# RMS normalisation on one core: the first three tiles' loads move to ScalarE's DMA queue, in few large transfers

## The chip, the core and the metric

The kernel runs on one core of a Trainium2 chip. A core has engines that run side by side, each with its own stream of instructions: TensorE (PE in the profile), VectorE (DVE), ScalarE (ACT), GpSimd (POOL) and SyncE (SP). SyncE does no arithmetic here: it issues transfers between the chip's memory (HBM) and the core's own memory (SBUF). ScalarE can issue transfers too, between its arithmetic. All transfers are carried by 16 DMA engines. The metric is the device time of one execution in microseconds (us).

## The reference

The input `x` has 16 x 1024 rows of 512 numbers in float32, 33.6 MB; the output has the same size. Every row is divided by its root mean square and multiplied by `gamma`, a vector of 512 numbers:

```python
eps = 1e-5
rms = np.sqrt(np.mean(x ** 2, axis=-1, keepdims=True) + eps)
return (x / rms * gamma).astype(np.float32)
```

## The kernel before

The 16384 rows are cut into four tiles of 4096: 128 partitions with 32 rows each. The rows of one partition are neighbours in HBM, so a transfer of 16 rows of each partition (half a tile, 4 MB) is made of 128 pieces of 32 KB. There are three buffers in SBUF (`slots`), each of one whole tile. Tiles 0, 1 and 2 have one each; tile 3 goes into tile 0's slot, and its loads wait until tile 0's stores have read that slot. Results overwrite the input in its slot and are stored from there.

The work goes by groups of rows, mostly half tiles. For a group:

- ScalarE squares its rows in pieces (L96) and VectorE sums each piece (L97) into `ss`. The pieces go in turn to a buffer in PSUM of seven rows and one in SBUF of five. A piece of nine rows, used for the first three half tiles, is squared into rows 23 to 31 of slot 2, whose own load comes late.
- ScalarE takes the root of the mean (L102), VectorE the reciprocal (L103).
- GpSimd takes the last `share` rows, seven of 16 mostly, and multiplies them by the reciprocal (L109) and by gamma (L110).
- ScalarE multiplies the other rows by the reciprocal, one instruction a row (L118), and VectorE multiplies them by gamma (L122).

The order on every engine is the order in which the kernel is written (`manual_schedule`). While group k is scaled, ScalarE already squares group k+1: two pieces ahead of the first half of its scaling, the rest between the halves. At the start, TensorE spreads gamma over the partitions with a matrix product (L66) and ScalarE copies it to SBUF (L165).

Before the change, SyncE issues every transfer, and its queue carries them out in the order of issue. It starts with row 0 of tile 0, rows 1 to 7, gamma in five pieces, rows 8 to 15, rows 16 to 31, and the first half of tile 1. Everything else is issued by `transfers`, after the group that is named there: after group (0, 0), stores of one row alternate with the second half of tile 1 and rows 0 to 22 of tile 2; after group (0, 16), which comes with both halves of tile 0 done, the rest of tile 2's load, the stores of tile 0 and the loads of tile 3. A store waits for VectorE's and GpSimd's products; a load into a slot that is still in use waits for the store from it. An issue that waits holds up those behind it on SyncE. L34 holds an address alignment of ScalarE's instructions, at the very start of its stream; L72 is a first activation that brings in ScalarE's table.

Of the kernel before, what the change touches and what calls it, by code (L numbers as in the profile page):

```python
# [9 lines left out]
def kernel(  # L10
# [6 lines left out]
    nc = tc.nc  # L17
    P = nc.NUM_PARTITIONS
    eps = 1e-5
    fp32 = mybir.dt.float32  # L20
# [5 lines left out]
    N, D = xf.shape  # L26
# [3 lines left out]
    xv = xf.rearrange("(t p r) d -> t p r d", p=P, r=R)  # L30
# [5 lines left out]
    const = ctx.enter_context(tc.tile_pool(name="const", bufs=1))  # L36
    stats = ctx.enter_context(tc.tile_pool(name="stats", bufs=9))
    psum = ctx.enter_context(tc.tile_pool(name="psum", bufs=1, space=bass.MemoryType.PSUM))

    slots = [const.tile([P, R, D], fp32, name=f"slot{i}") for i in range(3)]  # L40
# [1 line left out]
    before_scale = []  # L42

    def load(t, slot, r0, r1):
        dma = nc.sync.dma_start(out=slots[slot][:, r0:r1], in_=xv[t][:, r0:r1])  # L45
        before_scale.append((slot, r0, r1, dma))

    def store(t, slot, r0, r1):
        dma = nc.sync.dma_start(out=ov[t][:, r0:r1], in_=slots[slot][:, r0:r1])
        before_scale.append((slot, r0, r1, dma))  # L50

    gamma_row = const.tile([1, D], fp32)
    pieces = (0, 128, 224, 320, 416, D)

    load(0, 0, 0, 1)
    load(0, 0, 1, 8)
    for c0, c1 in zip(pieces, pieces[1:]):
        nc.sync.dma_start(out=gamma_row[:, c0:c1], in_=gamma.unsqueeze(0)[:, c0:c1])
    load(0, 0, 8, 16)
    load(0, 0, 16, 32)  # L60
    load(1, 1, 0, 16)

    ones_col = const.tile([1, P], fp32)
    nc.gpsimd.memset(ones_col, 1.0)  # L64
# [9 lines left out]


    groups = [
        (0, 0, 7, (7,), 3),
        (0, 7, 9, (9,), 5),
        (0, 16, 16, (7, 9), 7),
        (1, 0, 16, (7, 9), 7),  # L80
        (1, 16, 16, (7, 5, 4), 7),
        (2, 0, 16, (7, 5, 4), 7),
        (2, 16, 16, (7, 5, 4), 7),
# [3 lines left out]
    slot_of = [0, 1, 2, 0]  # L87

    def square_sums(ss, t, g, r, m, k):
        if m == 9:  # L90
            sq = slots[2][:, 23:32, :]
        else:
            home, name, most = ((psum, "sq_psum", 7), (const, "sq_sbuf", 5))[k % 2]
            sq = home.tile([P, most, D], fp32, name=name)
        rows = slots[slot_of[t]][:, g + r : g + r + m, :]
        nc.scalar.activation(out=sq[:, :m], in_=rows, func=AF.Square)  # L96
        nc.vector.tensor_reduce(  # L97
            out=ss[:, r : r + m, 0], in_=sq[:, :m], axis=mybir.AxisListType.X, op=OP.add
        )
# [28 lines left out]

    def transfers(t, g):
        if (t, g) == (0, 0):  # L130
            store(0, 0, 0, 1)
            load(1, 1, 16, 32)
            store(0, 0, 1, 2)
            load(2, 2, 0, 23)
        elif (t, g) == (0, 16):
            store(0, 0, 2, 3)
            load(2, 2, 23, 32)
            store(0, 0, 3, 16)
            store(0, 0, 16, 32)
            load(3, 0, 0, 16)  # L140
            load(3, 0, 16, 32)
        elif (t, g) == (1, 16):
            store(1, 1, 0, 32)
        elif (t, g) == (2, 16):
            store(2, 2, 0, 32)
        elif (t, g) == (3, 0):
            store(3, 0, 0, 16)
        elif (t, g) == (3, 16):
            store(3, 0, 16, 32)
# [12 lines left out]
    for piece in todo:  # L162
        square_sums(*piece)
    rstd = inverse_rms(ss, groups[0][2])
    nc.scalar.copy(out=gamma_b[:, 0], in_=gamma_psum[:, 0])  # L165
    for k, group in enumerate(groups):
        t, g, n, pieces, share = group
        mine = n - share
        half = (mine + 1) // 2
        ahead = groups[k + 1 :][:1]  # L170
        ss, todo = pieces_of(ahead[0]) if ahead else (None, [])
        scale_by_pool(rstd, t, g, n, share)
        for piece in todo[:2]:
            square_sums(*piece)
        scale(rstd, t, g, 0, half)
        for piece in todo[2:]:
            square_sums(*piece)
        scale(rstd, t, g, half, mine)
        times_gamma(t, g, 0, mine)
        transfers(t, g)  # L180
        for nxt in ahead:
            rstd = inverse_rms(ss, nxt[2])
# [30 lines left out]
```

## Time and profile before

| what | value |
|---|---|
| device time, median of 3 runs | 161.59 us (161.41 to 161.67) |
| the profiled execution's own time, as recorded: its span, first to last instruction | 160.2 us |
| the median over that span | 1.4 us |
| VectorE, ScalarE, GpSimd busy | 112.0, 107.8, 106.4 us (70%, 67%, 66%) |
| TensorE busy | 2.0 us |
| moved by DMA | 67.12 MB, 419 GB/s over the span |

For the profiled execution the record has no device time apart from its span, so sums are made against the span and the 1.4 us is added. In the profile, a name such as L97 is line 97 of the kernel. A group's row shows the instruction, the tile written and the tiles read, the count, and behind the bar the busy time in us and the mean of one in ns, then the engine's idle time before them and what ended it. A "q" behind an engine's name (SPq) is its sequencer, which issues transfers and waits. A row of the timeline begins with start and length in us. In the table by stage, each engine's busy time comes with its number of instructions, and the last three columns are the granted TensorE clock, the DMA engines' share and the GB/s moved.

### The profile page before, as it was taken

Reading aid. Unit: us, or ns where it says so; the run is one execution under the profiler, and the core shown is the slowest. Engines: PE = TensorE matmul, PEld = TensorE weight load, DVE = VectorE, ACT = ScalarE, POOL = GpSimd, SP = SyncE. Lnnn points to the kernel's source line nnn. Section 1 sums busy time; section 2 is a strip of 40 time slices with the busy share of each in tenths; the row PEclk is TensorE's granted clock in tenths of the full one; section 3 lists DMA queues with packets and bytes.
Section 4 is the critical chain, followed back from the end, with each engine's and each line's share of the span. In section 5 each row is a group of like instructions: output and inputs, shape, how many; then the busy total and the mean of one; then the engine's idle time right before and its main releaser. Section 6 shows DMA issues by size and latency. Waiting matters only on the chain.

```text
span 160.2 us, 276 instructions
## 1 busy us (share of the span) xinstructions
PE 2.0 (1%) x2; PEld 0.5 (0%) x2; DVE 112.0 (70%) x39; ACT 107.8 (67%) x108; POOL 106.4 (66%) x24
## 2 busy tenths in 40 slices
PE   0050000000000000000000000000000000000000
PEld 0010000000000000000000000000000000000000
DVE  0018098899798999999999999999999009700000
ACT  3071967976999998999899899989960990000000
POOL 1000951994999599999999999999999980000000
DMA  5999999899999899999999999996996996999994
GB/s 189 431 421 475 442 401 458 340 446 491 417 435 494 388 379 383 426 450 475 434 401 426 483 401 393 524 491 295 524 491 295 524 491 295 401 491 417 401 450 196
DMA packets 2747, 67.12 MB, mean 419 GB/s; under 512 B 313, under 2 KB 314, under 8 KB 826
## 3 DMA queue, kind: packets, MB, share of 16 engines
q1 hardware_dynamic: 2746, 67.11, 98.1%
q14 instruction: 1, 0.01, 0.0%
HBM read 33.56 MB, written 33.55 MB: 419 GB/s over the span
## 4 chain that ended last, share of the span: by engine, by line
DVE 59%; ACT 22%; DMA 4%; ACTq 0%; issue 0%; SPq 0%
DVE ss L97 36%; DVE slot L122 23%; ACT slot L118 8%; ACT slot L96 7%; ACT sq_psum L96 6%; DMA slot<-in_x_dram 4%; DVE ss L103 1%; ACT ss L102 1%; ACTq L208 0%; ACT gamma_b L165 0%; SPq L45 0%; ACTq L96 0%
## 5 line engine op out<-in xcount | busy, mean ns | idle before, releaser
L109 POOL TENSOR_TENSOR slot<-slot,ss 128x3584 f32<-128x3584 f32 (+2 forms) x9 | 47.0, 5218 | 24.1 <-DVE ss L103 24.1
L110 POOL TENSOR_TENSOR slot<-slot,gamma_b 128x3584 f32<-128x3584 f32 (+2 forms) x9 | 59.3, 6587 | 0.7
L97 DVE TENSOR_REDUCE ss<-sq_psum 128x7 f32<-128x3584 f32 (+1 forms) x13 | 42.2, 3247 | 13.7 <-ACT sq_psum L96 13.7
L118 ACT ACTIVATE slot<-slot,ss 128x512 f32<-128x512 f32 x75 | 47.3, 706 | 4.7 <-DVE ss L103 4.7
L122 DVE TENSOR_TENSOR slot<-slot,gamma_psum 128x4608 f32<-128x4608 f32 (+2 forms) x9 | 41.3, 4590 | 8.7 <-ACT slot L118 8.7
L96 ACT ACTIVATE sq_psum<-slot 128x3584 f32<-128x3584 f32 (+1 forms) x13 | 34.6, 2658 | 6.4 <-DMA slot<-in_x_dram 5.7
L97 DVE TENSOR_REDUCE ss<-slot 128x9 f32<-128x4608 f32 x3 | 14.9, 4954 | 4.4 <-ACT slot L96 4.2
L97 DVE TENSOR_REDUCE ss<-sq_sbuf 128x5 f32<-128x2560 f32 x5 | 14.0, 2803 | 0.0
L96 ACT ACTIVATE slot<-slot 128x4608 f32<-128x4608 f32 x3 | 12.1, 4033 | 0.0
L96 ACT ACTIVATE sq_sbuf<-slot 128x2560 f32<-128x2560 f32 x5 | 11.6, 2321 | 0.0
L102 ACT ACTIVATE ss<-ss,eps_t 128x16 f32<-128x16 f32 (+2 forms) x9 | 2.7, 305 | 11.9 <-DVE ss L97 11.9
L103 DVE RECIPROCAL ss<-ss 128x16 f32<-128x16 f32 (+2 forms) x9 | 2.1, 236 | 0.4 <-ACT ss L102 0.4
L66 PE MATMUL gamma_psum<-gamma_row,ones_col 1*128 1x512 f32 x2 | 2.0, 1122 | 8.6 <-DMA gamma_row<-in_gamma_dram 8.6
L72 ACT ACT_TABLE_LOAD x1 | 1.3, 1283 | 1.2 <-PEq L197 1.2
L165 ACT COPY gamma_b<-gamma_psum 128x512 f32<-128x512 f32 x1 | 0.6, 567 | 0.0
L66 PEld LDWEIGHTS gamma_psum<-gamma_row,ones_col 1*128 1x128 f32 x2 | 0.5, 308 | 8.6 <-issue 8.6
L64 POOL MEMSET ones_col<- 1x128 f32 x1 | 0.2, 195 | 0.3 <-POOLq L197 0.3
L197 POOL MEMSET const-float32-0.0<- 128x1 f32 x1 | 0.1, 99 | 0.2 <-issue 0.2
L72 ACT ACTIVATE table<-eps_t 128x1 f32<-128x1 f32 x1 | 0.2, 202 | 0.0
L197 POOL MEMSET const-bfloat16-1.0<- 128x1 bf16 x1 | 0.1, 102 | 0.0
L197 POOL MEMSET const-uint8-127<- 128x1 uint8 x1 | 0.1, 102 | 0.0
L197 POOL MEMSET const-float32-1.0<- 128x1 f32 x1 | 0.1, 99 | 0.0
(1 smaller groups left out, 0.1 us busy)
## 6 DMA issues: line engine op xcount, KB each, us to landing
slot<-in_x_dram SPq DMA_DIRECT2D x5, 4096.0 KB, 21.9
out_dram<-slot SPq DMA_DIRECT2D x3, 4096.0 KB, 23.4
slot<-in_x_dram SPq DMA_DIRECT2D x1, 5888.0 KB
out_dram<-slot SPq DMA_DIRECT2D x1, 3328.0 KB, 21.8
slot<-in_x_dram SPq DMA_DIRECT2D x1, 2304.0 KB, 14.3
slot<-in_x_dram SPq DMA_DIRECT2D x1, 2048.0 KB, 9.9
slot<-in_x_dram SPq DMA_DIRECT2D x1, 1792.0 KB, 7.0
out_dram<-slot SPq DMA_DIRECT2D x3, 256.0 KB
```

The source lines that it names most:

```text
L66: nc.tensor.matmul(gamma_psum[:, 0], ones_col, gamma_row, start=True, stop=True)
L72: nc.scalar.activation(out=table, in_=eps_t, func=AF.Sqrt)
L96: nc.scalar.activation(out=sq[:, :m], in_=rows, func=AF.Square)
L97: nc.vector.tensor_reduce(out=ss[:, r : r + m, 0], in_=sq[:, :m], axis=mybir.AxisListType.X, op=OP.add)
L102: nc.scalar.activation(out=ss[:, :n, 0], in_=ss[:, :n, 0], func=AF.Sqrt, bias=eps_t, scale=1.0 / D)
L103: nc.vector.reciprocal(out=ss[:, :n, 0], in_=ss[:, :n, 0])
L109: nc.gpsimd.tensor_tensor(out=part, in0=part, in1=by_row, op=OP.mult)
L110: last = nc.gpsimd.tensor_tensor(out=part, in0=part, in1=gamma_b.to_broadcast([P, share, D]), op=OP.mult)
L118: nc.scalar.activation(out=x[:, g + r, :], in_=x[:, g + r, :], func=AF.Copy, scale=rstd[:, r])
L122: scaled = nc.vector.tensor_tensor(out=part, in0=part, in1=gamma_psum.to_broadcast([P, r1 - r0, D]), op=OP.mult)
L165: nc.scalar.copy(out=gamma_b[:, 0], in_=gamma_psum[:, 0])
L197: nc = _bacc.Bacc("TRN2", target_bir_lowering=False, num_devices=1)
```

## The change

The loads of tiles 0, 1 and 2 are issued by ScalarE, five in a row at the start of its stream: two halves of tile 0, the whole of tile 1 at once (8 MB), two halves of tile 2. SyncE keeps gamma, now in one piece, all stores, and the loads of tile 3. The stores of single rows are gone, and so are the small first loads: tile 0's first half is one group of 16 rows, and all groups but the last have the same form, squared in pieces of 7, 5 and 4 rows. Slot 2 is no longer lent to squares.

```diff
     def load(t, slot, r0, r1):
-        dma = nc.sync.dma_start(out=slots[slot][:, r0:r1], in_=xv[t][:, r0:r1])
+        queue = nc.sync if t == 3 else nc.scalar
+        dma = queue.dma_start(out=slots[slot][:, r0:r1], in_=xv[t][:, r0:r1])
         before_scale.append((slot, r0, r1, dma))
...
-    pieces = (0, 128, 224, 320, 416, D)
-
-    load(0, 0, 0, 1)
-    load(0, 0, 1, 8)
-    for c0, c1 in zip(pieces, pieces[1:]):
-        nc.sync.dma_start(out=gamma_row[:, c0:c1], in_=gamma.unsqueeze(0)[:, c0:c1])
-    load(0, 0, 8, 16)
+    load(0, 0, 0, 16)
+    nc.sync.dma_start(out=gamma_row, in_=gamma.unsqueeze(0))
     load(0, 0, 16, 32)
-    load(1, 1, 0, 16)
+    load(1, 1, 0, 32)
+    load(2, 2, 0, 16)
+    load(2, 2, 16, 32)
...
-        (0, 0, 7, (7,), 3),
-        (0, 7, 9, (9,), 5),
-        (0, 16, 16, (7, 9), 7),
-        (1, 0, 16, (7, 9), 7),
+        (0, 0, 16, (7, 5, 4), 7),
+        (0, 16, 16, (7, 5, 4), 7),
+        (1, 0, 16, (7, 5, 4), 7),
         (1, 16, 16, (7, 5, 4), 7),
...
-        if m == 9:
-            sq = slots[2][:, 23:32, :]
-        else:
-            home, name, most = ((psum, "sq_psum", 7), (const, "sq_sbuf", 5))[k % 2]
-            sq = home.tile([P, most, D], fp32, name=name)
+        home, name, most = ((psum, "sq_psum", 7), (const, "sq_sbuf", 5))[k % 2]
+        sq = home.tile([P, most, D], fp32, name=name)
...
         if (t, g) == (0, 0):
-            store(0, 0, 0, 1)
-            load(1, 1, 16, 32)
-            store(0, 0, 1, 2)
-            load(2, 2, 0, 23)
+            store(0, 0, 0, 16)
         elif (t, g) == (0, 16):
-            store(0, 0, 2, 3)
-            load(2, 2, 23, 32)
-            store(0, 0, 3, 16)
             store(0, 0, 16, 32)
             load(3, 0, 0, 16)
             load(3, 0, 16, 32)
```

## The prediction

> **What bounds the kernel now.** I began with the page's row of DMA by slice and its table of DMA queues, to see whether the transfers or the engines set the end.
>
> ```profile
> span 160.2 us, 276 instructions
> DMA  5999999899999899999999999996996996999994
> DMA packets 2747, 67.12 MB, mean 419 GB/s; under 512 B 313, under 2 KB 314, under 8 KB 826
> q1 hardware_dynamic: 2746, 67.11, 98.1%
> ```
>
> All transfers lie on one queue, and their packets fill 98.1% of 16 engines' span: 157.2 of 160.2 us. The sixes late in the row are no gaps: a 64 KB packet lasts 2.4 us and is booked whole in one slice, so neighbours read over and under one. Longer stretches, from the table by stage, show the pace:
>
> ```profile
> 1.50:4.00 2.50, 0.00 (x0) 0.00 (x0) 0.00 (x0) 1.14 (x2) 0.00 (x0) 1.00 0.89 303
> 4.00:10.00 6.00, 1.36 (x2) 0.50 (x2) 0.00 (x0) 1.69 (x1) 0.00 (x0) 1.00 1.02 427
> 64.00:84.00 20.00, 0.00 (x0) 0.00 (x0) 20.00 (x9) 19.16 (x17) 19.92 (x4) 1.00 1.01 437
> 100.00:140.00 40.00, 0.00 (x0) 0.00 (x0) 31.00 (x11) 26.00 (x33) 31.57 (x6) 1.00 1.00 433
> 140.00:158.00 18.00, 0.00 (x0) 0.00 (x0) 0.00 (x0) 0.00 (x0) 0.00 (x0) 1.00 1.01 435
> ```
>
> The last two columns are the DMA share and GB/s. From 140 us no compute engine works at all, and the transfers run on at 435. The pace is 433 GB/s whether the stretch holds loads, stores or both, and only the start falls short (303). So the bytes at 433 are worth 155.0 us; everything else is where the stream starts, what small packets waste, and about 1.2 us of tail (last packet at 159.0, last landing 159.34, then the closing barrier of 0.8). The chain that ended last names VectorE for 59%, but VectorE is late for nothing: its last product ends at 139.1, when the queue still holds work until 149. What compute must do is hand over each store before the queue runs dry.
>
> The issuing side, from the timeline, SyncE's waits and the waits of the engines:
>
> ```profile
> 0.74 0.86 SPq L45 DMA_DIRECT2D slot<-in_x_dram  x2
> 1.15 1.28 ACT L72 ACT_TABLE_LOAD   x1 [1.15 <-PEq L197]
> 8.31 3.16 ACT L96 ACTIVATE sq_psum<-slot 128x3584 f32<-128x3584 f32 x1 [5.66 <-DMA slot<-in_x_dram]
> SPq L45 <- DMA slot<-in_x_dram: 4.2, 1, 4.2
> ```
>
> SyncE issues its first load at 0.74; ScalarE's first instruction starts only at 1.15 (a branch, from the address alignment at L34, lies at 0.74). SyncE's wait of 4.2 us is a landing semaphore used again: eight take turns in the trace's DMA records, and the tenth transfer needs the second's.
>
> The pace of compute, from the groups by form (mean ns):
>
> ```profile
> L97 DVE TENSOR_REDUCE ss<-sq_psum 128x7 f32<-128x3584 f32 x8 | 30.8, 3852 | 13.7 <-ACT sq_psum L96 13.7
> L97 DVE TENSOR_REDUCE ss<-sq_sbuf 128x5 f32<-128x2560 f32 x5 | 14.0, 2803 | 0.0
> L97 DVE TENSOR_REDUCE ss<-sq_psum 128x4 f32<-128x2048 f32 x5 | 11.4, 2280 | 0.0
> L122 DVE TENSOR_TENSOR slot<-slot,gamma_psum 128x4608 f32<-128x4608 f32 x6 | 29.7, 4945 | 0.6 <-ACT slot L118 0.6
> L110 POOL TENSOR_TENSOR slot<-slot,gamma_b 128x3584 f32<-128x3584 f32 x6 | 46.8, 7799 | 0.5
> L109 POOL TENSOR_TENSOR slot<-slot,ss 128x3584 f32<-128x3584 f32 x6 | 37.0, 6169 | 3.8 <-DVE ss L103 3.8
> ```
>
> A half tile costs GpSimd 6.17 + 7.80 = 13.97 us; VectorE's cycle in the timeline is 13.68 (inverse at 69.0, 82.7, 96.4).
>
> **The change, part by part.** The sum is made against the profiled span, 160.2; the median of the runs is 161.59, so 1.4 us is added at the end for what lies around the span.
>
> *Start of the stream.* The first load leaves ScalarE at about 1.15 instead of SyncE at 0.74: +0.41 us. The first packet came 1.0 after its issue, so now at 2.16. Bounds: 0 (if the branch vanishes) to 1.7 (if the table load of 1.28 came first; it stands at L72, behind the loads, so I don't take that).
>
> *Few large transfers.* In the packet records, the 512 packets of 2 KB took 2.95 us of the 16 engines' time, 0.53 more than their bytes at 433; the 14 KB ones 0.27 more; completion records, 24 transfers before and 14 after, 0.06. Most of the first two falls in the opening four microseconds, where any first transfer may be slow. So the gain is from 0.25 (only the later 2 KB stores, odd sizes and records) to 0.85 (all); I take 0.45, near the middle since the first packets, of 2 KB, are slow in part for being first. Other slow packets, reads near 29, 61 and 98 us, worth about 0.9, belong to no size and stay.
>
> *ScalarE's order.* Five issues of some 0.4 us ahead of the table load move it to 3.2 and its end to 4.5. Cover: the first rows land at about 12.8. Without that cover the move would cost 2.1 us. Six transfers precede the first store, fewer than eight semaphores, so no load waits for one; the later ones reuse those of transfers long landed. SyncE issues gamma at 0.74 instead of behind two loads; its matmul (8.6) gates nothing before the copy at 15.6: 0. One gamma transfer for five frees 1.2 us of SyncE, which then waits anyhow: 0.
>
> *Compute starts later.* The first half tile is 4.19 MB: 2.16 + 0.6 for a slow start + 9.7 + 0.4 to landing = 12.8 (8.2 now, for eight rows). ScalarE's first square 3.14 to 16.0, three reductions 3.85 + 2.80 + 2.28 to 24.9, root and reciprocal to 25.4. Next ScalarE does copy, squares and nine scales, 0.5 + 7.34 + 9 x 0.63, to 38.9, VectorE's product 4.94, and the first store goes at 43.9 (now 27.4). The whole of tile 1 lands together, 16.8 MB in: 2.8 + 38.7 + 0.4 = 41.9, so ScalarE, ready at 39.2, waits 2.7; inverse of group 2 at 60.0. Then 13.68 each: 73.7, 87.4, 101.1, 114.7, 128.4. The last half takes 15.5 from its inverse to its store (123.67 to 139.2): 143.9. GpSimd, at 13.97, ends tile 1 at 88.1, tile 2 at 116.0, the first half of tile 3 at 130.0.
>
> Against it the queue: loads of three tiles, tile 0's stores and tile 3's loads are 41.9 MB, 96.9 us, done at 99.7; tile 1's store until 119.0, tile 2's until 138.4, then 148.1 and 157.8. Stores arrive at 88.1, 116.0, 130.0 and 143.9, each a microsecond before its first packet. The thinnest cover is 2.0 us at tile 2, then 3.2 at the end. So the late start is hidden: 0; gone, it costs what compute is late beyond 2 us, one for one. The regrouping (7, 9 to 7, 5, 4) adds 8.93 - 8.80 = 0.13 us of VectorE a half tile, inside the same cover.
>
> *Two queues at once.* From 45 us, when the first store meets the loads still queued (15 us of them), until about 80, both queues hold work and each engine can alternate reads and writes. The trace has one queue only. Nearest rows: tile 3's first load follows a store and lands 9.7 us after it, the 9.7 of its bytes; tile 1's store lands 19.4 after a load, where its bytes need 19.36. So a turn costs 0 to 0.05 us. An engine moves 29 packets of 1.21 us in 35 us: 29 turns, 0 to 1.5 us. I take 0.4, below the middle, since an engine's records show 0.006 us between the last packet of a load and the first of a store behind it; not less, because here all engines read and write at once for long, which no row shows. From below, a gain: over 16 us or more only two stretches pass 437 GB/s, each beside a slower one into which packets are booked differently (446 in 10 to 26 before 362 in 26 to 32; 456 in 32 to 50 before 384), so no more than 1% is likely, 0.35.
>
> The Trainium skill, DMA: Bandwidth & Descriptors, section "Issuing engines are not separate DMA queues", holds that transfers from any issuing engine run on the same 16 DMA engines and interleave, and that several issuers save only issue time. This trace, with one issuer, can't show it; taken literally the two queues cost and bring 0, and the sum would be 161.55. It speaks against the change: SyncE's issues are hidden already. That page's "Queues, rings and completion order" adds turns by packet between the rows; by it the halves would be even.
>
> *Sum.* 160.2 + 0.41 - 0.45 + 0.4 = 160.6, with the 1.4 around it **162.0**; the price of the turns is the loosest term. From term bounds: 160.2 + 0 - 0.85 + 0 to 160.2 + 0.41 - 0.25 + 1.5, so 160.8 to 163.3.
>
> **The rivals.**
>
> *Faster: the small packets' whole loss goes and turns are free.* 160.2 + 0.41 - 0.85 = 159.8, or 161.2 with the rest; about 160.6 if mixing also gains 1 to 2% of 35 us. For: turns on one queue cost next to nothing. Against: the start is late in any case, and first packets are slow. It decides when turns cost under 0.1 us in all.
>
> *Reads and writes held together run slower.* At 5% less over 35 us of queue work 1.8 us, at 10% 3.9: 163.4 to 165.5. For: every stretch at 433 is nearly pure. Against: the free turns.
>
> *Stores crowd out the loads.* The second half of tile 2 lands, with even turns, at 45 + 2 x 15.3 = 76 and is needed by ScalarE at 82. If stores get two thirds, it lands near 88.5; compute is 6 late, 2 are covered: some 4 more, 166. It starts below a share of about 0.4. For: SyncE's queue never empties there. Against: equal 32 KB packets on both.
>
> *ScalarE held by its own issues.* Should the third or fifth load wait for room, its first square would be late, until the thinnest cover of 2 us breaks: 163 if held 3 us past 12.8. Against: SyncE put out 8 MB in 0.34 us with more than 4 MB queued.
>
> **How the numbers follow.** A measurement can tell about 0.2% from no change: 161.27 to 161.91 counts as none. My case has 0.52 (own range 161.2 to 163.0; 0.03 of it faster, 0.17 none, 0.32 slower); the faster rival 0.20 (0.19 faster, 0.01 none); slow mixing 0.17; crowding 0.06; a held ScalarE 0.05, the last three slower. Faster 0.22, none 0.18, slower 0.60. For 8 in 10 the range takes the likeliest case, most of the faster one and half of slow mixing: 160.8 to 164.4.
>
> **What would show it.** First issue on ScalarE at 1.15, first packet at 2.2; first square near 12.8; a ScalarE wait for a load of 2 to 3 us at 39 to 42; stores issued at 44, 60, 88, 116, 130 and 144; two DMA queues in the table with a total share near 98%; 430 GB/s in 45 to 80. Wrong: a later first issue, under 415 GB/s in 45 to 80, slices of DMA below nine in a row after 100, or a long ScalarE wait near 82.

## The result, and the profile after

The changed kernel takes 164.42 us in the median of four runs (164.03 to 164.58), against 161.60 before (161.41 to 161.67): 1.0169 times as long, with a 95% interval of 1.0154 to 1.0183. The forecast of slower was right in sign; its 162.0 was 2.4 us too low, and the median lies 0.02 us above the upper end of the range, 164.4. Some executions take 1% or more longer than the rest of the same kernel; the ratios compare only runs within 1.5% of the fastest of their kernel.

The page of the changed kernel, its span and its DMA rows:

```profile
span 162.2 us, 255 instructions
DMA  1899996995999999989989989959959959899895
DMA packets 1875, 67.12 MB, mean 414 GB/s; under 512 B 209, under 2 KB 209, under 8 KB 210
q1 hardware_dynamic: 1154, 41.95, 59.9%
q10 hardware_dynamic: 720, 25.17, 36.9%
q14 instruction: 1, 0.01, 0.0%
```

ScalarE's queue (q10) and SyncE's (q1) together fill 96.8% of the span, 157.0 us; before, one queue filled 98.1%, 157.2 us. So the transfers need the same time as before, and the 2 us are time without transfers. The first slice of the DMA row says where: a 1 stands where a 5 stood. The timeline's first rows (start and length in us):

```profile
0.74 0.34 SPq L55 DMA_DIRECT2D gamma_row<-in_gamma_dram  x1
1.17 4.15 ACTq L46 DMA_DIRECT2D slot<-in_x_dram  x5
5.35 1.28 ACT L70 ACT_TABLE_LOAD   x1 [5.35 <-issue]
15.02 3.16 ACT L90 ACTIVATE sq_psum<-slot 128x3584 f32<-128x3584 f32 x1 [8.18 <-DMA slot<-in_x_dram]
```

And the same kernel's load line with its issues (min/median/max in ns, then first and last start in us):

```profile
L46 ACTq DMA_DIRECT2D slot<-in_x_dram x5: 448/462/2134, 1.2 to 4.9; - x5
```

Of ScalarE's five issues, four take some 0.46 us; the first takes 2.13. In the trace's packet records the first packet of the rows is at 3.93 us, before at 1.75: 2.18 us later. From the end of the first issue to the first packet it is 0.63 us in both kernels, so the delay lies in the issue and in what stands ahead of it. The first square follows at 15.0. The spans differ by 2.1 us (162.25 and 160.17), and the late first packet covers all of that.

The rest of the stream, first by the table by stage (the last two columns are the DMA share and GB/s). The kernel after:

```profile
45.00:80.00 35.00, 0.00 (x0) 0.00 (x0) 32.70 (x14) 33.98 (x34) 31.84 (x5) 1.00 1.00 419
100.00:140.00 40.00, 0.00 (x0) 0.00 (x0) 31.86 (x13) 32.46 (x39) 38.02 (x7) 1.00 1.03 445
```

And the kernel before, in the first of these stretches:

```profile
45.00:80.00 35.00, 0.00 (x0) 0.00 (x0) 34.44 (x12) 33.42 (x37) 33.15 (x6) 1.00 0.99 422
```

Then by SyncE's rows in the timeline of the kernel after:

```profile
45.53 16.64 SPq L50 DMA_DIRECT2D out_dram<-slot  x2
69.27 15.33 SPq L46 DMA_DIRECT2D slot<-in_x_dram  x2
90.11 55.89 SPq L50 DMA_DIRECT2D out_dram<-slot  x4
```

The stores of tile 2 and of the last two halves of tile 3 go out at 118.1, 132.1 and 145.7 (the trace's issue records). The transfers before them begin to land at 122.2, 141.5 and 151.2. The queue never runs dry, so late compute costs nothing directly. While both queues hold work, the rate is 419 GB/s; in the same stretch the one queue of the kernel before moved 422, so this rate tells nothing of two queues.

One more difference appears in the run records. Time less span is 1.7 to 1.8 us in every run of either kernel. Before, runs of 161.4 to 161.6 us have spans of 159.6 to 159.8, so the profiled 160.2 belongs to a run some 0.4 us slower than its median. Medians are therefore compared below: 2.8 us are to be explained, 2.18 of them by the start.

### The profile page after: what moved, and what is told of

Read it like the earlier page. It is cut to its first block, busy times and chain, and to the rows that moved or that the text cites. A ratio compares the mean times of both kernels' runs of the same rounds, so it can differ in the third digit from the quotient of the medians.

```text
span 162.2 us, 255 instructions
## 1 busy us (share of the span) xinstructions
PE 2.0 (1%) x2; PEld 0.5 (0%) x2; DVE 112.6 (69%) x40; ACT 108.5 (67%) x111; POOL 104.1 (64%) x22
## 4 chain that ended last, share of the span: by engine, by line
DVE 50%; DMA 25%; ACT 12%; ACTq 2%; issue 0%
DVE ss L91 27%; DMA slot<-in_x_dram 25%; DVE slot L116 22%; ACT slot L112 8%; ACT sq_psum L90 3%; ACTq L46 2%; ACT sq_sbuf L90 1%; DVE ss L97 1%; ACTq L196 0%; ACTq L34 0%
## 5 line engine op out<-in xcount | busy, mean ns | idle before, releaser
L103 POOL TENSOR_TENSOR slot<-slot,ss 128x3584 f32<-128x3584 f32 (+1 forms) x8 | 45.9, 5735 | 33.0 <-DVE ss L97 33.0
L91 DVE TENSOR_REDUCE ss<-sq_psum 128x7 f32<-128x3584 f32 (+1 forms) x16 | 49.1, 3069 | 24.1 <-ACT sq_psum L90 24.1
L104 POOL TENSOR_TENSOR slot<-slot,gamma_b 128x3584 f32<-128x3584 f32 (+1 forms) x8 | 58.0, 7246 | 0.6
L112 ACT ACTIVATE slot<-slot,ss 128x512 f32<-128x512 f32 x76 | 48.0, 706 | 4.7 <-DVE ss L97 4.7
L90 ACT ACTIVATE sq_psum<-slot 128x3584 f32<-128x3584 f32 (+1 forms) x16 | 40.2, 2512 | 14.0 <-DMA slot<-in_x_dram 11.6
L116 DVE TENSOR_TENSOR slot<-slot,gamma_psum 128x4608 f32<-128x4608 f32 (+1 forms) x8 | 41.7, 5216 | 8.5 <-ACT slot L112 8.5
L91 DVE TENSOR_REDUCE ss<-sq_sbuf 128x5 f32<-128x2560 f32 x8 | 22.4, 2806 | 0.0
L90 ACT ACTIVATE sq_sbuf<-slot 128x2560 f32<-128x2560 f32 x8 | 18.6, 2320 | 0.0
L96 ACT ACTIVATE ss<-ss,eps_t 128x16 f32<-128x16 f32 x8 | 2.4, 304 | 5.8 <-DVE ss L91 5.8
L97 DVE RECIPROCAL ss<-ss 128x16 f32<-128x16 f32 x8 | 2.0, 248 | 0.4 <-ACT ss L96 0.4
```

The source lines that it names most:

```text
L91: nc.vector.tensor_reduce(out=ss[:, r : r + m, 0], in_=sq[:, :m], axis=mybir.AxisListType.X, op=OP.add)
L96: nc.scalar.activation(out=ss[:, :n, 0], in_=ss[:, :n, 0], func=AF.Sqrt, bias=eps_t, scale=1.0 / D)
L97: nc.vector.reciprocal(out=ss[:, :n, 0], in_=ss[:, :n, 0])
L103: nc.gpsimd.tensor_tensor(out=part, in0=part, in1=by_row, op=OP.mult)
L104: last = nc.gpsimd.tensor_tensor(out=part, in0=part, in1=gamma_b.to_broadcast([P, share, D]), op=OP.mult)
L112: nc.scalar.activation(out=x[:, g + r, :], in_=x[:, g + r, :], func=AF.Copy, scale=rstd[:, r])
```

## The experiments

Theory A: the loss is the late start, a price of ScalarE's first issue. Against it: late compute or large first transfers (B), the size of the first transfer (C), two queues at once (D). What was left after that gave rise to theories E to H.

**One queue.** The kernel after the change, all loads from SyncE.

```diff
-        queue = nc.sync if t == 3 else nc.scalar
+        queue = nc.sync
```

> The kernel after the change, with the three tiles' loads issued by SyncE again; the large transfers, groups and late compute stay. Theory A (the loss is the start: ScalarE's first issue takes 2.1 us, so the whole stream starts 2.2 us late; late compute and large transfers cost nothing): first packet near 1.75, span 159.6 to 160.3, time 161.0 to 161.7. Theory B (late compute or the large first load costs): 163 to 164.5. Theory C (the size of the first load makes its issue slow): SyncE's first issue takes about 2 us too, time near 163.6. Two queues at once are gone as well, so this run alone doesn't tell A from a price of two queues.

Measured: 162.18 us (161.93 to 162.57), ratio to the kernel before 1.0038 (1.0024 to 1.0052). SyncE's first issue, of the same 4 MB, takes 0.38 us:

```profile
0.73 0.38 SPq L46 DMA_DIRECT2D slot<-in_x_dram  x1
1.17 0.31 SPq L55 DMA_DIRECT2D gamma_row<-in_gamma_dram  x1
1.53 2.14 SPq L46 DMA_DIRECT2D slot<-in_x_dram  x4
```

That is the single queue's timeline, SyncE alone. Size (C) falls, and B as the cause of the whole: 2.2 of the 2.8 us are gone. But 0.6 to 0.7 us stay, more than theory A's 161.0 to 161.7 allows.

**First load on SyncE, the others on ScalarE.**

```diff
-        queue = nc.sync if t == 3 else nc.scalar
+        queue = nc.sync if t == 3 or (t, r0) == (0, 0) else nc.scalar
```

> The kernel after the change, with only the first half tile's load on SyncE, the other four still on ScalarE. Theory A (late start): ScalarE's 2.1 us are covered by the first load's 10 us; first packet near 1.75, time within 0.4 us of the one-queue run, 161.0 to 162.0. Theory D (two queues at once cost: a halt of about 1 us where the stores join, and slower turns): 1 to 2 us above the one-queue run, 162.5 to 163.5.

Measured: 163.21 us (162.95 to 163.94), ratio 1.0103 (1.0078 to 1.0128). By the ranges this looks like theory D, but the trace has another reason (timeline, ScalarE's rows and SyncE's):

```profile
1.17 4.33 ACTq L46 DMA_DIRECT2D slot<-in_x_dram  x4
5.53 1.28 ACT L70 ACT_TABLE_LOAD   x1 [5.53 <-issue]
6.82 0.20 ACT L70 ACTIVATE table<-eps_t 128x1 f32<-128x1 f32 x1
19.31 3.16 ACT L90 ACTIVATE sq_psum<-slot 128x3584 f32<-128x3584 f32 x1 [12.28 <-DMA slot<-in_x_dram]
...
49.82 14.58 SPq L50 DMA_DIRECT2D out_dram<-slot  x2
72.56 10.11 SPq L46 DMA_DIRECT2D slot<-in_x_dram  x2
92.05 55.59 SPq L50 DMA_DIRECT2D out_dram<-slot  x4
```

The first packet is back at 1.75, but ScalarE's loads share the engines with the first half tile, which has landed on all engines only at 19.3 us, where the single queue had it at 12.95. Compute starts 6 us later, and tile 2's store is issued at 120.05, when tile 1's has begun to finish (119.96 to 121.62, engine by engine): the queue runs dry. Time inside the stream that no packet fills is about 1.4 us here and 0.4 with one queue (first to last packet, less the packets' mean time per engine). So this run does not price the alternation in the middle; it shows what a broken cover costs.

**Only gamma on ScalarE.** The kernel before, with gamma's five pieces issued by ScalarE.

```diff
-        nc.sync.dma_start(out=gamma_row[:, c0:c1], in_=gamma.unsqueeze(0)[:, c0:c1])
+        nc.scalar.dma_start(out=gamma_row[:, c0:c1], in_=gamma.unsqueeze(0)[:, c0:c1])
```

> The kernel before the change, with the five pieces of gamma issued by ScalarE: ScalarE's first issue is 512 bytes, and nothing waits for it before 8 us. Theory A with a price per first use: the first issue takes about 2.1 us, the other four 0.25 to 0.5; span 160 to 160.3. Theory C (size): the first issue takes 0.3 to 0.5. If the use of a second queue also costs time around the span, the time over the span is 1.8 instead of 1.4 us or less, and the time 161.9 to 162.2; otherwise 161.3 to 161.7.

Measured: 161.48 us (ratio 0.9997, 0.9964 to 1.0030), so no cost of a second queue around the span shows. The issues by line:

```profile
L58 ACTq DMA_DIRECT2D gamma_row<-in_gamma_dram x5: 223/270/2529, 1.2 to 4.6; - x5
```

512 bytes need 2.53 us where their neighbours need 0.27: the price belongs to the first issue, whatever its size.

**The start alone.** The kernel before, with its five first loads on ScalarE.

```diff
-        dma = nc.sync.dma_start(out=slots[slot][:, r0:r1], in_=xv[t][:, r0:r1])
+        queue = nc.scalar if (t, r0) in ((0, 0), (0, 1), (0, 8), (0, 16), (1, 0)) else nc.sync
+        dma = queue.dma_start(out=slots[slot][:, r0:r1], in_=xv[t][:, r0:r1])
```

> The kernel before the change, with its five first loads issued by ScalarE and all else by SyncE: small first transfers, compute as early as the start allows, no second queue at work later. Theory A: first packet of the rows near 3.9, span 162.0 to 162.6, time 163.5 to 164.5. Theories B and D (late compute or two queues at once made the loss): span within 0.5 of 160.2 plus ScalarE's later first instruction, 160.6 to 161.0, time 162.0 to 162.5.

Measured: ratio 1.0192 (1.0142 to 1.0242), a wide interval: the four runs compared are 163.63 to 165.01 us, of six up to 166.46. The profiled span, that of the fastest run, is 161.7, under theory A's 162.0 to 162.6; the first packet of the rows is at 3.93, as theory A has it.

```profile
L46 ACTq DMA_DIRECT2D slot<-in_x_dram x5: 335/450/2123, 1.2 to 6.0; - x5
```

No large transfers, no groups of 16 rows at the start, no second queue at work later: the late start alone makes a loss of 2 us or more. Theory A stands; what makes the first issue long was still open.

**Table first.** The kernel after, with the activation that loads ScalarE's table moved ahead of the loads.

```diff
+    eps_t = const.tile([P, 1], fp32)
+    nc.gpsimd.memset(eps_t, eps)
+    table = const.tile([P, 1], fp32)
+    nc.scalar.activation(out=table, in_=eps_t, func=AF.Sqrt)
     load(0, 0, 0, 16)
...
-    eps_t = const.tile([P, 1], fp32)
-    nc.gpsimd.memset(eps_t, eps)
-    table = const.tile([P, 1], fp32)
-    nc.scalar.activation(out=table, in_=eps_t, func=AF.Sqrt)
```

> The kernel after the change, with ScalarE's table load and first activation moved ahead of its five loads. Theory A1 (some 2.1 us belong to the first issue itself): the table load runs at 1.15, the first issue starts near 2.65, ends near 4.8, first packet of the rows near 5.4; 1.5 us above the kernel after, time 165.6 to 166.2. Theory A2 (the first issue waits for something that is ready at a fixed moment, such as an instruction block fetched at 1.8): the issue ends near 3.3 to 3.6 in spite of its late start, time within 0.4 us of the kernel after, 164.2 to 164.9.

Measured: 164.54 us (164.33 to 164.68), as the kernel after.

```profile
1.17 1.28 ACT L58 ACT_TABLE_LOAD   x1 [1.17 <-PEq L187]
1.23 2.29 ACTq L46 DMA_DIRECT2D slot<-in_x_dram  x1
2.46 0.20 ACT L58 ACTIVATE table<-eps_t 128x1 f32<-128x1 f32 x1
```

The issue begins at 1.23, beside the table load: ScalarE's sequencer goes on while the engine loads its table. Both theories had taken the two for one after the other, so the run doesn't tell them apart; it shows that here a table load in front does not cost its 1.28 us: the first packet of the rows comes at 4.16, 0.23 later than in the kernel after.

**Without the alignment.** The kernel after, without the line at the start of ScalarE's stream.

```diff
-    nc.scalar.addr_align(128, offset=0, max_nops=0)
```

> The kernel after the change without the address alignment at the start of ScalarE's stream. Theory A1: the first issue starts near 0.74 instead of 1.17 and still lasts about 2.1 us, first packet near 3.5, time 0.4 us below the kernel after, 163.8 to 164.2. Theory A3 (the branch of the alignment makes the sequencer fetch its code, and that is the 2.1 us): the issue lasts 0.4 us, first packet at 1.75 to 2.2, time 162.2 to 162.7. Where ScalarE runs out of fetched code later, up to 1 us of its stalls hide in the cover of 3 to 5 us.

Measured: 162.17 us (162.07 to 162.25), ratio 1.0031 (1.0021 to 1.0042). The timeline:

```profile
0.73 2.43 ACTq L45 DMA_DIRECT2D slot<-in_x_dram  x5
3.19 1.28 ACT L69 ACT_TABLE_LOAD   x1 [3.19 <-issue]
```

The load line's issues:

```profile
L45 ACTq DMA_DIRECT2D slot<-in_x_dram x5: 387/455/552, 0.7 to 2.7; - x5
```

And the page's row of the instruction queue, which had 1 packet in the kernel after:

```profile
q14 instruction: 2, 0.01, 0.0%
```

The first issue starts at 0.73 and takes 0.39 us; the first packet of the rows is at 1.76 (the one at 1.65 is gamma's). All of the start's price hung on the alignment and its branch: 0.43 us until the first issue, 1.7 in the issue itself. Of the two packets of instructions one has 32 bytes, at 0.17 us; the other, of 8 KB, comes at 64 us. In the aligned kernels the 8 KB packet comes near 1.8 us, inside the long issue. In the five of them in which ScalarE issues first, it ends at 2.17, 2.26, 2.37, 2.56 and 2.93 us, and the issue at 3.29, 3.30, 3.53, 3.71 and 4.02: 1.0 to 1.2 us later each time, while the issue's length goes from 2.12 to 2.84. So the issue seems to wait for that packet, and its end, not a fixed price, sets the first packet of the rows. That is argued and not shown: the records don't say whose code the packet holds, no run moves it by itself, and not everything behind the branch waits for it. In the kernel before, ScalarE's table load runs from 1.15 and its first activation from 2.45, and the packet ends only at 2.53.

The run also prices two queues, since its stream starts where that of the one-queue kernel does (first packets of the rows at 1.76 and 1.75): 162.17 us with two, 162.18 with one, or by the ratios to the kernel before 1.0031 and 1.0038. They cost and bring nothing beyond the intervals, some 0.3 us either way. In both the stretch from 45 to 80 is slower than 433, as it was before the change (422). Its row in the table by stage, without the alignment (with one queue the same stretch has 418):

```profile
45.00:80.00 35.00, 0.00 (x0) 0.00 (x0) 34.18 (x13) 33.99 (x36) 32.52 (x5) 1.00 0.99 420
```

**What the remaining 0.6 us are.** In the packet records of all these kernels, load packets take longer than their usual 1.21 us (32 KB) in one or two waves a few microseconds ahead of the first store's packets. The time over the usual, summed and divided by the 16 engines, from 20 to 70 us (of the profiled run), and the medians of all runs:

```
kernel                                       slow packets, us   median, us
before                                              0.65          161.51
before, gamma on ScalarE                            0.59          161.48
before, large start                                 0.47          161.64
one queue, early turn                               0.64          161.45
one queue, two early turns                          0.55          161.88
one queue, first store cut                          0.99          162.02
before, without single-row stores                   1.02          162.09
two queues, no alignment                            1.03          162.17
two queues, no alignment, first store cut           1.05          162.02
one queue                                           1.17          162.18
```

The kernel after itself, with the late start on top, has 1.05 us of them. The prediction had seen such packets in the trace of before (reads near 29, 61 and 98 us, worth about 0.9) and let them stay as they were.

**First store cut.** The one-queue kernel.

```diff
-            store(0, 0, 0, 16)
+            store(0, 0, 0, 1)
+            store(0, 0, 1, 16)
```

> The one-queue kernel, with the first store cut into one row and 15 rows, issued at the same moment. In the one-queue run two waves of load packets just ahead of the first 4 MB store take 1.17 us of all engines' time more than usual; ahead of the first single-row store of the kernel before it is 0.2 to 0.3. Theory E (the size of the first store makes that loss): the loss falls to 0.3 to 0.6, time 161.4 to 161.8. Theory F (the turn from loads to stores costs by itself, or by the depth of loads queued): unchanged near 1.1 us, time 162.0 to 162.4.

Measured: 162.02 us, ratio 1.0016 (0.9992 to 1.0040), and 0.99 us of slow packets. A small first store alone (E) doesn't take the loss away; but the 15 rows follow on its heels, so the queue turns to 4 MB of stores all the same.

**Early turn.** The one-queue kernel, with a load between the two stores.

```diff
     load(2, 2, 0, 16)
-    load(2, 2, 16, 32)
...
-            store(0, 0, 0, 16)
+            store(0, 0, 0, 1)
+            load(2, 2, 16, 32)
+            store(0, 0, 1, 16)
```

> The one-queue kernel, with the second half of tile 2 issued only behind a first store of one row, and the other 15 rows' store behind that load: as in the kernel before, the first turn from loads to stores is a small one with loads behind it. Theory G (the loss of about 1 us ahead of the first 4 MB store shrinks when a small store has made the first turn earlier): slow load packets ahead of both turns together 0.3 to 0.7 us of all engines' time, time 161.5 to 161.8. Theory F (it belongs to the first large store): about 1 us still, ahead of the store of 15 rows, time 162.0 to 162.3.

Measured: 161.45 us (161.31 to 161.74), ratio 0.9985 (0.9960 to 1.0011), 0.7 below the one-queue kernel; the slowest of these runs is faster than the fastest of those (161.93). SyncE's rows in the timeline:

```profile
43.38 0.35 SPq L50 DMA_DIRECT2D out_dram<-slot  x1
43.77 0.43 SPq L46 DMA_DIRECT2D slot<-in_x_dram  x1
44.30 15.80 SPq L50 DMA_DIRECT2D out_dram<-slot  x2
```

Compute is as late as ever (first store at 43.4); only the order in the queue differs. Slow packets: about 0.3 us ahead of the small store, 0.35 ahead of the large one. Theory G's numbers hold (the time is 0.05 below its range).

**One turn, early compute.** The kernel before, without its single-row stores.

```diff
     load(1, 1, 0, 16)
+    load(1, 1, 16, 32)
+    load(2, 2, 0, 23)
...
-        if (t, g) == (0, 0):
-            store(0, 0, 0, 1)
-            load(1, 1, 16, 32)
-            store(0, 0, 1, 2)
-            load(2, 2, 0, 23)
-        elif (t, g) == (0, 16):
-            store(0, 0, 2, 3)
+        if (t, g) == (0, 16):
             load(2, 2, 23, 32)
-            store(0, 0, 3, 16)
+            store(0, 0, 0, 16)
```

> The kernel before the change without its three single-row stores: the second half of tile 1 and rows 0 to 22 of tile 2 are issued at the start, tile 0 is stored in two halves; compute and the small first loads stay as before. Theories F and G: one turn from many queued loads to a 4 MB store, about 1 us of slow load packets ahead of it, time 161.9 to 162.3 in spite of early compute. Theory H (late compute or the large first load, not the turn, makes the one-queue kernel's 0.6 us): loss ahead of the turn 0.3 to 0.4, time 161.2 to 161.5.

Measured: 162.09 us (161.86 to 162.31), though the ratio is loose: 1.0021 (0.9994 to 1.0047), since three of the 29 runs of before beside it took 162.3 to 163.4; none of the other 26 is above 161.67, and all 12 here are. 1.02 us of slow packets. Taking the small turns out of the kernel before makes the same loss, with early compute: H falls. The one-queue kernel, with late compute, larger first transfers and the new groups besides, is at 162.18; so those cost no more than the runs can tell.

**Large start.** The kernel before, with rows 0 to 7 in one load and gamma in one piece.

```diff
-    load(0, 0, 0, 1)
-    load(0, 0, 1, 8)
-    for c0, c1 in zip(pieces, pieces[1:]):
-        nc.sync.dma_start(out=gamma_row[:, c0:c1], in_=gamma.unsqueeze(0)[:, c0:c1])
+    load(0, 0, 0, 8)
+    nc.sync.dma_start(out=gamma_row, in_=gamma.unsqueeze(0))
```

> The kernel before the change with its start made of fewer transfers: rows 0 to 7 in one load, gamma in one piece, all on SyncE. If small first transfers cost what the prediction took (up to 0.85 us for all of them, half of it at the start): 161.1 to 161.4. If the start is slow whatever its size, as the equal landings of the first half tile in the one-queue run suggest: 161.4 to 161.6.

Measured: 161.64 us, ratio 1.0003 (0.9972 to 1.0033). Nothing gained: the first packets are slow whatever their size (in the first 10 us of every kernel here, 0.5 to 0.7 us more than their bytes at 433 GB/s).

**Two early turns.** The early-turn kernel with one more.

```diff
             store(0, 0, 0, 1)
-            load(2, 2, 16, 32)
-            store(0, 0, 1, 16)
+            load(2, 2, 16, 24)
+            store(0, 0, 1, 2)
+            load(2, 2, 24, 32)
+            store(0, 0, 2, 16)
```

> The one-queue kernel with the early turn, with two single-row stores instead of one between the parts of tile 2's last load. If each small turn takes more off the loss ahead of the large store (0.36 us there in the run with one): slow load packets 0.3 to 0.5 us in all, time 161.1 to 161.4, below the kernel before. If two turns cost what one does, or the single rows' own packets eat it: 161.4 to 161.6.

Measured: 161.88 us, ratio 1.0038 (1.0015 to 1.0060): above both ranges, and slower than with one turn, though its slow packets are fewer. Two things weaken the comparison. About 0.15 of the 0.4 us lies outside the span (time less span is 1.9 to 2.0 here). And the trace is of a run of 162.99 us, in which one DMA engine's last packet ends 1.1 us after those of the other 15. Why a second small turn is no gain stays open; slow packets ahead of the turn may not be the whole price of an order.

**Two queues, both causes.** The kernel after without the alignment, and with the first store cut.

```diff
-    nc.scalar.addr_align(128, offset=0, max_nops=0)
...
-            store(0, 0, 0, 16)
+            store(0, 0, 0, 1)
         elif (t, g) == (0, 16):
+            store(0, 0, 1, 16)
             store(0, 0, 16, 32)
```

> The kernel after the change with both causes taken away as far as the runs name them, and two queues kept: no address alignment, and the first store is one row at its old moment, with the other 15 rows stored after the next half tile, when the loads on ScalarE's queue are nearly through. Theory G on two queues: slow load packets where the first store joins fall from 1.03 us to 0.3 to 0.7, time 161.4 to 161.8. If on two queues the join costs the same whatever the first store's size: 162.0 to 162.3.

Measured: 162.02 us, ratio 1.0028 (1.0019 to 1.0038). The edit missed its aim: the 15 rows' store waited for nothing, and SyncE issued it at 43.76, right behind the single row at 43.29, instead of at 60. It is the cut store again, with no gain that the runs can tell (162.17 without the cut), and leaves open whether an early turn would help on two queues.

No version beats the kernel before by more than the runs can tell; the early turn, at 161.45, equals it with simpler groups.

## Why the prediction was right and wrong

- **Start of the stream, +0.41:** the step that failed. The first issue did begin at 1.17, where the prediction put it. But the prediction took the issue's length, and the microsecond to the first packet, from SyncE's row. ScalarE's first issue behind the alignment's branch took 2.13 us, and the first packet came at 3.93, not 2.16: +2.18. The bound of 1.7 from above was built on the table load, which in front costs some 0.2; the branch, which the prediction had named, was priced only by the 0.41 that the trace of before showed. And the sum of the bounds left even the 1.7 out: it used 0.41 at its upper end, 163.3; with 1.7 it would have reached 164.6. The trace of before had no issue on ScalarE, so the bound should have been left open upwards there.
- **Few large transfers, -0.45:** wrong in size and, in sum, in sign. At the start they bring nothing (161.64 with a large start against 161.51 for the runs beside it). And with the single-row stores went the early turn: some 0.6 us lost, by two edits in opposite directions (early turn put in: -0.7; turns taken out: +0.6). The prediction saw the single-row stores as cost alone, and held the slow reads to be the same in either order.
- **Two queues at once, +0.4:** 0 by the kernel without the alignment and the one-queue kernel (162.17 and 162.18), within some 0.3 us. The Trainium skill's "DMA: Bandwidth & Descriptors", section "Issuing engines are not separate DMA queues", says that several issuing engines share the same 16 DMA engines and save only issue time. This pair agrees, within the same 0.3 us. That rule's sum, 161.55, missed for the same reason as mine: it says nothing of a late first issue.
- **Late compute, 0:** right. The prediction had the first square at 12.8 and the stores at 43.9, 88.1, 116.0 and 143.9; with one queue the stores are at 43.5, 88.1, 116.0 and 143.6, the first half tile has landed at 12.95, and the queue held work throughout. The thinnest cover, from the issue of tile 2's store to the first landing of tile 1's, was 4 us (116.0 against 120.0); less the microsecond that the prediction takes off for the first packet, 3 instead of its 2.0. Where the first tile's loads came over two queues, tile 2's store was 4 us later, just past that cover, and the queue ran dry for about 1 us.
- **Around the span, 1.4:** it is 1.8 in nearly every run, and 1.9 to 2.0 in three of the variants; the profiled run of before was slower than its median. As medians only are compared, the forecast used a span too long and a rest too short, and the two errors cancel in the sum.
- **The rivals:** reads and writes held together (5% slower) did not happen beyond the slow waves; the crowded loads did not either: 76 was forecast for the second half of tile 2, and it lands at 76.4 to 76.9 without the alignment (the rival's own sum was off: with a third of the pace left to the loads, 45 + 3 x 15.3 is 90.9, not 88.5). ScalarE was held by its own issue, but at its first one, with the stream itself late, and not by room in the queue.
- **The sign and the range:** luck, for the most part. Slower came out of +0.41 for the start, a fifth of what it cost, and +0.4 for turns that cost nothing that the runs can tell, against a gain of 0.45 that was a loss. The range reached up to 164.4 only because half of the slow-mixing rival was taken in, and that rival did not happen; the late start brought the time to the same place. Of the signs that it named, the first packet (3.93, not 2.2) and the first square (15.0, not 12.8) told; a later first issue, its sign of being wrong, did not come, since the issue began on time and was only longer.

In sum of medians: 161.5 before, +0.7 for the order and the rest of the change on one queue (0.6 of it the order), 0.0 for two queues, +2.25 for the branch at the head of ScalarE's stream: 164.4.

## What to carry to other kernels

When the first transfer of a kernel moves to another engine, look at what that engine's stream does before it: the issue stands behind the engine's own prologue, and in a kernel bound by its transfers the delay is paid in full (here 2.18 us of late start and 2.25 of time). A row of an issue on one engine does not price the first issue on another; where the trace has none, one cheap run with a tiny transfer moved over measures it (gamma here: 2.53 us for 512 bytes). A small transfer that looks like waste may set the order of reads and writes in the queue; take it out by itself before calling it overhead.

## What the runs showed of the hardware that was not expected

- The first DMA issue on ScalarE behind the alignment's branch took 2.12 to 2.84 us in five kernels, for 512 bytes as for 4 MB; without the alignment 0.39. The later ones took some 0.22 to 0.55. The end of this issue comes 1.0 to 1.2 us after the end of an 8 KB packet of instructions in all five.
- ScalarE's sequencer issued a transfer at 1.23 us while the table load of 1.28 us, ahead of it in the stream, was running from 1.17.
- Load packets slow down ahead of a turn to stores, by 1.0 to 1.2 us of all engines' time with one large turn, 0.5 to 0.65 where a store of one row had made a turn with loads behind it. Why is open: neither the first store's size alone (a cut store still loses 0.99) nor the number of turns (two take 161.88 us, one 161.45) explains all of it.
